# A seven-product form for one more projection of an encoder trunk, and a new order of the kernel's last five stages

## The chip, the cores and the metric

The kernel runs on one core of a Trainium2 chip. The metric is the time on the device, in microseconds (us), as the median of several runs. The engines are TensorE (PE, matrix products), VectorE (DVE, element-wise work), ScalarE (ACT, element-wise work and copies), GpSimd (POOL) and SyncE (SP, which issues all the transfers here).

## What is computed

One layer of a bidirectional encoder for a prompt of 1024 tokens and a sample of 512 tokens, 1024 channels, everything in 32-bit floats. `_hgrn2_bidir` is a gated linear recurrence in both directions over 8 heads of 128 channels, with a norm of each head.

```python
h = _rmsnorm(x, norm_g)
proj = jnp.einsum('bld,de->ble', h, w_in)
(q, f_fw, f_bw, i, z_a, c_B, c_C, c_x, z_b, g_a, g_b) = jnp.split(proj, SPLIT_POINTS, axis=-1)
o_a = _hgrn2_bidir(q, i, f_fw, f_bw, lb_fw, lb_bw, hnorm_g).astype(x.dtype)
p_a = jnp.einsum('ble,ed->bld', o_a * jax.nn.silu(z_a), w_a)
conv = _centred_short_conv(c_C * c_x, conv_w, conv_b)
p_b = jnp.einsum('ble,ed->bld', c_B * conv * jax.nn.silu(z_b), w_b)
merged = jax.nn.sigmoid(g_a) * p_a + jax.nn.sigmoid(g_b) * p_b
return x + jnp.einsum('bld,de->ble', merged, w_o)      # then a final RMSNorm
```

The first branch is `p_a` (weights `w_a`), the second `p_b` (weights `w_b`).

## The kernel before

**Products.** Each 32-bit operand is split into two parts of type fp32r: `split` (L61) has ACT copy the high part (`w_h` of a weight block, `s_h` of activations) and then DVE subtract it from the source (`w_l`, `s_l`). A product is three passes, high by high, high by low, low by high (`PASSES`, L34). A plain product of a block of 128 channels with 512 tokens is 8 x 3 = 24 matmuls of 128x512 into one bank of PSUM (`mm_channels`, L90, its matmul L94). A *unit* is one such product for the sample, with the loading and splitting of its weight block done up to three units ahead.

**Seven products for eight.** For two blocks of channels and two halves of the prompt (or, in the output, of the columns), `two_blocks` (L766) forms seven products of half the depth, 12 matmuls each (L781), in place of four whole ones (4 x 24). It needs sums of the weights (`S`, four DVE operations L792 to L797, then splits), and sums of the other operand: B11, B21 and B22 are quarters of it, T1 to T4 sums of quarters. Those seven are made once for a stage by `operands` (L709), four steps of loads, subtractions and splits, and lie in seven slots of SBUF (`s0` to `s6`), each a high and a low part. The products' sums are added on DVE (`c`, `sum`).

**The stages.** The norm, values and the prompt's projections take the first 885 us. Then comes the recurrence (the GLA loop, L662): for each of 8 heads three steps, the prompt's two blocks and the sample (`order`, L653). In a step PE computes the scores of the block before (`near_scores`, L447 its matmuls; `transpose_keys`, L496), while DVE, ACT and POOL make the decays of the next (`decays`, K and Q on L433 and L434, `cat` on L431 and L432). Between the pieces stand units of the sample's projections, three in each step (L678, L684, L689), so nine for a head. `outputs` (L521) uses a single bank of PSUM: matmuls L533, squares on ACT L537, a sum on DVE L538, a power on POOL, a scaling on ACT L541 that frees the bank. The prompt's outputs come in two halves, with one unit between them. The order of PE in the loop is that of the code.

After the loop, a `while` loop (L901) issues the units that are left, and between them the first steps of the next operands. The order from there, by a scheduler within each engine: the sample's `w_b` (plain), the prompt's `w_b` (seven products), the prompt's `w_a` (plain, two halves of 512 tokens for each of 8 blocks), the sample's `w_a` (plain), the output with `w_o` (seven products, six pairs of token blocks). In a plain stage `weights_ahead` (L815) loads and splits weight blocks three ahead and takes a step of the following stage's operands after every second block.

```python
        O = {n: slot(qp, i) for i, n in ((2, "T1"), (3, "T2"), (4, "T4"))}
        act = act_parts(cz_x[1], slot(qp, 5), slot(qp, 6))
        ...
        O |= {"B11": slot(keep, 0), "T3": slot(keep, 1)}
        ...
        O |= {"B21": slot(qp, 5), "B22": slot(qp, 6)}
```

Slots 0 and 1 (`keep`) hold the normed sample during the loop and the units behind it, so what is put there waits for the last of those units.

Of the kernel before, what the change touches and what calls it, by code (L numbers as in the profile page):

```python
# [10 lines left out]
F32 = mybir.dt.float32  # L11
# [3 lines left out]
ALU = mybir.AluOpType  # L15
# [3 lines left out]
P = 128  # L19
D = 1024  # L20
# [23 lines left out]
def trunk_kernel(ctx: ExitStack, tc: tile.TileContext, xs, w, outs, masks_d, ident_d):  # L44
# [330 lines left out]
    with outer:  # L375
# [286 lines left out]
        for i in range(len(order) + 1):  # L662
# [26 lines left out]
            unit()  # L689
# [16 lines left out]
        qp, io = opened(outer, "qp", bufs=1), opened(outer, "io", bufs=4)  # L706
# [50 lines left out]
        def products(O, srcs, use, early=False):  # L757
# [75 lines left out]
        def branch_b_prompt(O):  # L833
            s = {}

            def srcs(i):
                js = range(2 * i, min(2 * i + 2, NH))
                for j in js:
                    yield w["w_b"][:, j * P:(j + 1) * P].rearrange("(k p) c -> p k c", p=P)
                for j in js:  # L840
                    s[j] = io.tile([P, 2, TB], F32, name="io")
                    load(s[j].rearrange("p a b -> p (a b)"), gb_x[0][j])

            def use(i, m, t, c, more):
# [3 lines left out]
                V.tensor_tensor(s[m][:, t, :], u, s[m][:, t, :], op=ALU.mult)  # L848
                if m % 2 != t:
                    store(pb_x[0][m], s[m].rearrange("p a b -> p (a b)"))  # L850
# [3 lines left out]
        def branch_a(blocks, x, acts):  # L854
            n = len(acts)
            for j, whl in blocks:
                if n == 1:
                    both = io.tile([P, 2, TB], F32, name="io")
                    s, s2 = both[:, 0, :], both[:, 1, :]
                else:  # L860
                    s, s2 = (io.tile([P, n * TB], F32, name="io") for _ in range(2))
                load(s, ga_x[x][j])
                load(s2, pb_x[x][j])
                for t in range(n):
                    cols = slice(t * TB, (t + 1) * TB)
                    V.tensor_tensor(s[:, cols], plain(whl, acts[t]), s[:, cols], op=ALU.mult)
                V.tensor_tensor(s, s, s2, op=ALU.add)
                store(m_x[x][j], s)

        def output(O):  # L870
            xt, ss = {}, {}
# [9 lines left out]
            def use(i, m, h, c, more):  # L881
# [5 lines left out]
                if m != h:  # L887
# [7 lines left out]
            products(O, srcs, use, early=True)  # L895

        rows = lambda k: cz_x[0][k]
        O = {n: slot(qp, i) for i, n in ((2, "T1"), (3, "T2"), (4, "T4"))}
        act = act_parts(cz_x[1], slot(qp, 5), slot(qp, 6))
        steps = operands(O, tuple(O), rows)  # L900
# [6 lines left out]
        O |= {"B11": slot(keep, 0), "T3": slot(keep, 1)}  # L907
        blocks = weights_ahead("w_b", steps + operands(O, ("B11", "T3"), rows))
        next(blocks)
        branch_b_sample(blocks, act)  # L910
        O |= {"B21": slot(qp, 5), "B22": slot(qp, 6)}
        for step in operands(O, ("B21", "B22"), rows):
            step()
        stage = ExitStack()
        wk = opened(stage, "wk", bufs=1, side="right")
        branch_b_prompt(O)
        stage.close()

        xp = opened(stage, "xp", bufs=1, side="right")
        rows = lambda k: w["w_o"][k * P:(k + 1) * P, :]  # L920
        steps = []
        blocks = weights_ahead("w_a", steps)
        next(blocks)
        acts = [act_parts(oz_d[0], slot(keep, 0), slot(qp, 3)), act_parts(oz_d[1], slot(keep, 1), slot(qp, 2))]
        O = {"T4": slot(qp, 4), "T1": slot(qp, 5), "T2": slot(qp, 6)}
        steps += operands(O, tuple(O), rows)
        branch_a(blocks, 0, acts)
        steps = []
# [46 lines left out]
```

## Time and profile before

| | |
|---|---|
| median of 3 runs | 1977.19 us |
| lowest, highest | 1972.35, 1985.93 us |
| the profiled execution | 1982.88 us |
| its span in the trace | 1981.1 us |
| stages in the trace: GLA loop | 885 to 1576 us |
| units left over, `w_b` of the sample | 1576 to 1643 us |
| `w_b` of the prompt | 1643 to 1723 us |
| `w_a` of the prompt, of the sample | 1723 to 1811, to 1855 us |
| output | 1855 to 1981 us |

The profile is of one execution. Busy time of a matmul in it counts from its start to its modelled end, and matmuls overlap; the pitch, from one start to the next, is what a matmul costs. An engine's idle time is put down to the instruction that released it. A name such as `w_l<-w_raw,w_h` gives an instruction's output and inputs; the last three columns of a window are the clock granted to TensorE as a share of full speed, the busy share of the DMA engines and GB/s; `io` are tiles for loads and stores of stages, `pw` and `pp` PSUM banks.

### The profile page before, as it was taken

The page shows a single profiled execution, that of the slowest core. Times are in us where ns is not written, and L with a number is a line of the kernel's source. Part 1 is how long each engine was busy: PE and PEld are TensorE (multiplying, and loading weights), DVE is VectorE, ACT ScalarE, POOL GpSimd, SP SyncE. Part 2 cuts the span into 40 slices and gives each one's busy share as a digit, 9 for nine tenths or more (in the row PEclk, how much of TensorE's full clock was granted, in tenths as well). Part 3 has the DMA queues.
Part 4 walks back from the last instruction along what each step waited for, and adds up shares of the span by engine and source line. Part 5 has one row for each costly group of instructions (what it writes and reads, how often), then busy time and mean ns, then how long its engine had stood idle before and what let it go on. Part 6 is the DMA issues. An engine that isn't in the chain of part 4 may idle for free.

```text
span 1981.1 us, 37160 instructions
## 1 busy us (share of the span) xinstructions
PE 1940.3 (98%) x14820; PEld 1633.4 (82%) x14820; DVE 1476.4 (75%) x2369; ACT 981.5 (50%) x1956; POOL 170.2 (9%) x220
## 2 busy tenths in 40 slices
PE   9999999999999999998999999999999999999998
PEld 8988888888888888886888888888888887888786
DVE  6558686878676777776688878879788378765687
ACT  6433333343424333345677877877877443332332
POOL 1000000000000000003121322322212000000000
PEclk8999999999999999998999999999999999999999
DMA  7433333333324242435443534434333497798653
GB/s 214 146 108 103 115 96 107 102 120 97 120 88 131 77 138 75 128 113 184 146 124 118 161 112 128 142 106 156 110 120 104 143 308 254 241 313 278 214 186 107
DMA packets 313757, 288.85 MB, mean 146 GB/s; under 512 B 19184, under 2 KB 252912, under 8 KB 313584
## 3 DMA queue, kind: packets, MB, share of 16 engines
q1 hardware_dynamic: 313584, 286.49, 45.8%
q8 instruction: 116, 1.90, 0.4%
q14 instruction: 57, 0.47, 0.1%
HBM read 208.84 MB, written 77.59 MB: 145 GB/s over the span
## 4 chain that ended last, share of the span: by engine, by line
PE 77%; issue 9%; DVE 5%; DMA 5%; ACT 3%; POOL 1%; SPq 0%; DVEq 0%; POOLq 0%; ACTq 0%
PE pp L309 38%; PE pp L94 16%; PE pw L781 9%; PE pp L215 5%; PE o L533 2%; PE pp L87 2%; PE sc L447 2%; DMA io<-in_w_o 1%; PE u L509 1%; DVE Q L434 1%; DVE K L433 1%; ACT cat L431 1%; DVE w_l L64 1%; DMA w_raw<-in_w_b 1%; PE tp L177 1%
## 5 line engine op out<-in xcount | busy, mean ns | idle before, releaser
L309 PE MATMUL pp<-s_h,w_h 128*128 128x512 f32 x1120 | 435.9, 389 | 1.2 <-ACT w_h L63 1.2
L309 PE MATMUL pp<-s_l,w_h 128*128 128x512 f32 x1120 | 435.7, 389 | 0.0
L309 PE MATMUL pp<-s_h,w_l 128*128 128x512 f32 x1120 | 435.7, 389 | 0.0
L63 ACT ACTIVATE w_h<-w_raw 128x1024 fp32r<-128x1024 f32 (+1 forms) x250 | 209.6, 838 | 323.4 <-PE pp L309 137.8
L94 PE MATMUL pp<-s_h,w_h 128*128 128x512 f32 x896 | 356.5, 398 | 0.0
L94 PE MATMUL pp<-s_h,w_l 128*128 128x512 f32 x896 | 350.0, 391 | 1.5 <-DVE w_l L64 1.5
L94 PE MATMUL pp<-s_l,w_h 128*128 128x512 f32 x896 | 350.0, 391 | 0.2 <-DVE s_l L64 0.2
L64 DVE TENSOR_TENSOR w_l<-w_raw,w_h 128x1024 fp32r<-128x1024 f32 (+1 forms) x250 | 238.4, 954 | 101.0 <-ACT w_h L63 99.4
L314 DVE TENSOR_TENSOR tmp<-pp,tmp 128x512 f32<-128x512 f32 x240 | 165.3, 689 | 156.1 <-PE pp L309 156.1
L309 PEld LDWEIGHTS pp<-s_h,w_h 128*128 128x128 f32 x1120 | 210.2, 188 | 45.3 <-ACT w_h L63 1.8
L309 PEld LDWEIGHTS pp<-s_l,w_h 128*128 128x128 f32 x1120 | 210.2, 188 | 43.6
L309 PEld LDWEIGHTS pp<-s_h,w_l 128*128 128x128 f32 x1120 | 210.2, 188 | 43.6
L63 ACT ACTIVATE w_h<-w_S 128x512 fp32r<-128x512 f32 x160 | 101.0, 632 | 263.4 <-PE pp L309 263.3
L94 PEld LDWEIGHTS pp<-s_h,w_l 128*128 128x128 f32 x896 | 168.6, 188 | 38.3 <-DVE w_l L64 2.3
L94 PEld LDWEIGHTS pp<-s_l,w_h 128*128 128x128 f32 x896 | 168.9, 189 | 34.1 <-DVE s_l L64 1.0
L94 PEld LDWEIGHTS pp<-s_h,w_h 128*128 128x128 f32 x896 | 169.2, 189 | 33.0 <-ACT w_h L63 0.3
L431 ACT COPY cat<-K 128x512 f32<-128x512 f32 x168 | 111.6, 668 | 36.8 <-DVE K L433 35.4
L433 DVE TENSOR_TENSOR K<-K,T 128x512 f32<-128x512 f32 x144 | 110.1, 764 | 18.7 <-ACT cat L431 17.4
L432 ACT COPY cat<-Q 128x512 f32<-128x512 f32 x168 | 111.4, 668 | 19.4 <-DVE Q L434 10.8
L434 DVE TENSOR_TENSOR Q<-Q,T 128x512 f32<-128x512 f32 x144 | 104.0, 722 | 16.2 <-ACT cat L432 15.5
L781 PE MATMUL pw<-s_h,w_h 128*128 128x512 f32 x280 | 110.6, 395 | 2.5 <-ACT w_h L63 2.5
L781 PE MATMUL pw<-s_h,w_l 128*128 128x512 f32 x280 | 110.5, 395 | 1.1 <-DVE w_l L64 1.1
(178 smaller groups left out, 2961.5 us busy)
## 6 DMA issues: line engine op xcount, KB each, us to landing
w_raw<-in_w_in SPq DMA_DIRECT2D x166, 512.0 KB, 4.4
fkq_d<-sg SPq DMA_DIRECT2D x48, 256.0 KB, 2.3
io<-cz_p SPq DMA_DIRECT2D x20, 512.0 KB, 5.4
fkq_d<-sk SPq DMA_DIRECT2D x32, 256.0 KB, 2.1
F<-fkq_d SPq DMA_DIRECT2D x16, 512.0 KB, 3.7
K<-fkq_d SPq DMA_DIRECT2D x16, 512.0 KB, 6.5
w_raw<-in_w_b SPq DMA_DIRECT2D x16, 512.0 KB, 4.8
w_raw<-in_w_a SPq DMA_DIRECT2D x16, 512.0 KB, 6.1
```

The source lines that it names most:

```text
L63: A.activation(hi, src, AF.Copy)
L64: V.tensor_tensor(lo, src, hi.bitcast(F32), op=ALU.subtract)
L87: T.matmul(out, lhs(k, a), parts[k // 2][b][:, k % 2, :], start=k == 0 and n == 0, stop=k == KT - 1 and n == 2)
L94: T.matmul(out, whl[a][:, k, :], rhs(k, b), start=k == 0 and n == 0, stop=k == KT - 1 and n == 2)
L215: T.matmul(pp, B[f"B{k // 4 + 1}{t + 1}"][a][:, k % 4, c * P:(c + 1) * P], parts[k][b], start=k == 0 and m == 0, stop=k == KT - 1 and m == 2)
L309: T.matmul(bank, hl[x][:, k, :], B[b][y][:, k, :], start=k == 0 and i == 0, stop=k == 3 and i == 2)
L314: V.tensor_tensor(out, p, t, op=ALU.add)
L431: A.copy(ap(cat, 0, [[2 * hs, nb], [hs, 2], [1, hs]]), kall)
L432: A.copy(ap(cat, TB, [[2 * hs, nb], [hs, 2], [1, hs]]), qall)
L433: V.tensor_tensor(kall, kall, ap(t, m + 1, [[2, nb], [-m - 1, 2], [0, hs]]), op=ALU.mult)
L434: V.tensor_tensor(qall, qall, ap(t, 1, [[2, nb], [m - 1, 2], [0, hs]]), op=ALU.mult)
L781: T.matmul(bank, hl[x][:, c:c + P], O[n][y][:, k, :], start=k == 0 and i == 0, stop=k == 3 and i == 2)
```

## The change

1. The prompt's `w_a` takes the seven-product form: 4 pairs x 7 x 12 = 336 matmuls of 128x512, where 384 stood. Gate and second branch are applied to each half block (`branch_a_prompt`).
2. In the GLA loop the third unit of a step is left out in the sample's step (`i % 3 < 2`), so a head has eight units. The eight units go to the `while` loop behind it, which has 12 left where it had 4; the list of units is dealt out by fours accordingly.
3. The last five stages stand in this order: the prompt's `w_b`, the sample's `w_b`, the prompt's `w_a`, the sample's `w_a`, output. A seven-product stage has its first five operands (`FIRST`) made during the stage before and the last two (`LAST`: B21 and B22) at that stage's end, in slots that the stage before still reads.
4. In `two_blocks`, the product with B21 comes last but one in the first pair of a stage and second in the later ones; the output had it second in all, `w_b` last but two in all.
5. `io` has 8 tiles (4 before), `wk` is opened once, and the ring in SBUF for descriptors (`dynamic_dma_scratch_size`) is set to 2048.

```diff
-            units += [narrow(n, h) for n in ("q", "ff", "fb", "za")] + [wide(0)] * (h == 0) + later[5 * h:5 * h + 5]
-        units += later[5 * NH:]
+            units += [narrow(n, h) for n in ("q", "ff", "fb", "za")] + [wide(0)] * (h == 0) + later[4 * h:4 * h + 4]
+        units += later[4 * NH:]
...
-            unit()
+            if i % 3 < 2:
+                unit()
...
-        qp, io = opened(outer, "qp", bufs=1), opened(outer, "io", bufs=4)
+        qp, io = opened(outer, "qp", bufs=1), opened(outer, "io", bufs=8)
...
-                raws = two_blocks(O, *raws, partial(use, i), early, partial(srcs, i + 1))
+                raws = two_blocks(O, *raws, partial(use, i), i > 0, partial(srcs, i + 1))
...
+            use(1, 0, c21, prod(last, 0, "T4"))
             if not early:
                 use(0, 0, c11, prod(first, 1, "B21"))
-            use(1, 0, c21, prod(last, 0, "T4"))
             use(0, 1, c12, prod(s34, 1, "B22"))
...
+        def branch_prompt(name, O, finish_block, pb=None):
+
             s = {}
 
             def srcs(i):
                 js = range(2 * i, min(2 * i + 2, NH))
                 for j in js:
-                    yield w["w_b"][:, j * P:(j + 1) * P].rearrange("(k p) c -> p k c", p=P)
+                    yield w[name][:, j * P:(j + 1) * P].rearrange("(k p) c -> p k c", p=P)
                 for j in js:
                     s[j] = io.tile([P, 2, TB], F32, name="io")
-                    load(s[j].rearrange("p a b -> p (a b)"), gb_x[0][j])
+                    load(s[j].rearrange("p a b -> p (a b)"), (gb_x if name == "w_b" else ga_x)[0][j])
+                    if name == "w_a":
+                        pb[j] = io.tile([P, 2, TB], F32, name="io")
+                        load(pb[j].rearrange("p a b -> p (a b)"), pb_x[0][j])
...
+        def branch_a_prompt(O):
+            pb = {}
+
+            def block(m, t, s, u):
+                V.tensor_tensor(u, u, s[:, t, :], op=ALU.mult)
+                V.tensor_tensor(s[:, t, :], u, pb[m][:, t, :], op=ALU.add)
+                left_of[m] = left_of.get(m, 0) + 1
+                if left_of[m] == 2:
+                    store(m_x[0][m], s.rearrange("p a b -> p (a b)"))
+
+            left_of = {}
+            branch_prompt("w_a", O, block, pb)
...
+        FIRST, LAST = ("B11", "T1", "T2", "T3", "T4"), ("B21", "B22")
+        wk = None
+
+        def first_operands(slots, rows):
+            O = dict(zip(FIRST, slots))
+            return O, operands(O, FIRST, rows)
+
+        def last_operands(O, slots, rows):
+            O |= dict(zip(LAST, slots))
+            for step in operands(O, LAST, rows):
+                step()
...
         rows = lambda k: cz_x[0][k]
...
+        O, steps = first_operands(take(2, 3, 4, 5, 6), rows)
         while todo or ready:
             unit()
             if steps:
                 steps.pop(0)()
         order_pe.close()
         right.close()
...
+        wk = opened(outer, "wk", bufs=1, side="right")
+        fg = wk.tile([P, D], F32, name="fg")
+        load(fg, w["final_g"].to_broadcast([P, D]))
+        last_operands(O, take(0, 1), rows)
+        branch_b_prompt(O)
+
+        rows = lambda k: oz_x[0][k]
+        act = act_parts(cz_x[1], *take(2, 4))
+        O, steps = first_operands(take(5, 3, 6, 0, 1), rows)
+        blocks = weights_ahead("w_b", steps)
         next(blocks)
         branch_b_sample(blocks, act)
...
+        last_operands(O, take(2, 4), rows)
+        branch_a_prompt(O)
+
         rows = lambda k: w["w_o"][k * P:(k + 1) * P, :]
...
+        act = act_parts(oz_x[1], *take(5, 6))
+        O, steps = first_operands(take(0, 1, 2, 3, 4), rows)
         blocks = weights_ahead("w_a", steps)
         next(blocks)
...
+        branch_a_sample(blocks, act)
+        last_operands(O, take(5, 6), rows)
         output(O)
```

Two places show how instructions move. The first is ACT at the start of the output. `s0_h` to `s6_h` are the slots' high parts (of `w_o`'s operands), `io` the loaded rows of `w_o`, `S` the sums of the merged activations and `w_raw` those activations as loaded. Before:

```order
L63 ACTIVATE s0_h_18813<-io_19107 128x512 [waits DMAHW1_49]
L63 ACTIVATE s3_h_18817<-io_19109 128x512 [waits DMAHW3_49]
L63 ACTIVATE s2_h_18819<-io_19109 128x512
L63 ACTIVATE s1_h_18815<-io_19107 128x512 [waits DVE_49]
L63 ACTIVATE w_h_19208<-S_19167 128x1024 [waits DVE_49,PE_49,Activation_49]
L789 COPY c_19168<-pw_19175 128x512 [waits PE_49]
L63 ACTIVATE w_h_19228<-S_19167 128x1024 [waits DVE_49,Activation_49]
```

And after the change:

```order
L63 ACTIVATE s5_h_19235<-io_19239 128x512 [waits DMAHW1_49,PE_49]
L63 ACTIVATE s4_h_18865<-io_19188 128x512 [waits DVE_49]
L63 ACTIVATE s5_h_19235<-io_19245 128x512 [waits DMAHW2_49]
L63 ACTIVATE s5_h_19235<-io_19251 128x512 [waits DMAHW3_49]
L63 ACTIVATE s6_h_19237<-io_19239 128x512 [waits PE_49]
L63 ACTIVATE s6_h_19237<-io_19245 128x512
L63 ACTIVATE s6_h_19237<-io_19251 128x512
L63 ACTIVATE s5_h_19235<-io_19257 128x512 [waits DMAHW5_49]
L63 ACTIVATE s6_h_19237<-io_19257 128x512
L63 ACTIVATE w_h_19277<-w_raw_19263 128x1024 [waits DMAHW6_49,Activation_49]
L63 ACTIVATE w_h_19297<-S_19273 128x1024 [waits DVE_49,Activation_49]
L63 ACTIVATE w_h_19317<-S_19273 128x1024 [waits DVE_49,Activation_49]
```

Before, the first `w_h` of the output stood further ahead, and only splits for slots 0 to 3 came before the `w_h` of `S`; none of those splits waits for PE. Now eight splits for slots 5 and 6, B21 and B22, stand ahead of the first `w_h<-w_raw`, and the first for each slot waits for PE, which reads them as the sample's operand of `w_a`.

The second place is DVE at the start of the prompt's `w_b`, where slots hold parts of the second branch's `cz`, loaded into `io`. Before, at the end of the sample's `w_b` (L830 applies its gate):

```order
L64 TENSOR_TENSOR s0_l_17223<-io_17504,s0_h_17222 128x512 [waits DMAHW5_49,Activation_49]
L726 TENSOR_TENSOR io_17504<-io_17506,io_17504 128x512 [waits DMAHW7_49,DMAHW1_49]
L64 TENSOR_TENSOR s1_l_17225<-io_17504,s1_h_17224 128x512 [waits Activation_49]
L792 TENSOR_TENSOR S_17581<-w_raw_17575 128x512 [waits DMAHW0_49]
L796 TENSOR_TENSOR S_17581<-w_raw_17573,w_raw_17575 128x512
L793 TENSOR_TENSOR S_17581<-S_17581,w_raw_17573 128x512 [waits DVE_49]
L830 TENSOR_TENSOR io_17513<-pp_17515,io_17513 128x512 [waits DMAHW6_49,DMAHW2_49,PE_49]
L797 TENSOR_TENSOR S_17581<-w_raw_17573,S_17581 128x512 [waits DVE_49]
L64 TENSOR_TENSOR w_l_17606<-S_17581,w_h_17605 128x1024 [waits Activation_49]
```

And after the change, behind the units left over:

```order
L64 TENSOR_TENSOR s0_l_17224<-io_17245,s0_h_17223 128x512 [waits DMAHW2_49,Activation_49]
L64 TENSOR_TENSOR s1_l_17226<-io_17227,s1_h_17225 128x512 [waits PE_49,Activation_49]
L64 TENSOR_TENSOR s1_l_17226<-io_17233,s1_h_17225 128x512 [waits Activation_49]
L64 TENSOR_TENSOR s1_l_17226<-io_17239,s1_h_17225 128x512 [waits Activation_49]
L64 TENSOR_TENSOR s1_l_17226<-io_17245,s1_h_17225 128x512 [waits Activation_49]
L794 TENSOR_TENSOR S_17259<-w_raw_17253 128x512 [waits DMAHW7_49,Pool_49]
L798 TENSOR_TENSOR S_17259<-w_raw_17251,w_raw_17253 128x512
L795 TENSOR_TENSOR S_17259<-S_17259,w_raw_17251 128x512 [waits DVE_49]
L799 TENSOR_TENSOR S_17259<-w_raw_17251,S_17259 128x512 [waits DVE_49]
L64 TENSOR_TENSOR w_l_17284<-S_17259,w_h_17283 128x1024 [waits Activation_49]
```

Before, the `S` sums stood behind the last splits of slots 0 and 1 (B11 and T3) and ahead of the last gate of the sample, and slots 5 and 6 (B21, B22) came behind them. Now the splits of slots 0 and 1, which are B21 and B22 here, all stand ahead of the `S` sums, and those of slot 1 wait for PE's last unit.

## Rows read from the trace of the kernel before

**Rows 1.** The page: busy time, share and instructions of each engine.

```profile
PE 1940.3 (98%) x14820; PEld 1633.4 (82%) x14820; DVE 1476.4 (75%) x2369; ACT 981.5 (50%) x1956; POOL 170.2 (9%) x220
```

**Rows 2.** By stage: us; busy PE, PEld, DVE, ACT, POOL; clock, DMA share, GB/s.

```profile
885.00:1576.00 691.00, 669.12 (x8852) 566.94 (x8851) 536.21 (x883) 499.07 (x1152) 155.05 (x192) 0.98 0.43 132
...
1643.00:1723.00 80.00, 78.07 (x337) 63.85 (x336) 62.30 (x90) 29.52 (x42) 0.00 (x0) 0.98 0.67 227
...
1855.00:1981.00 126.00, 116.50 (x505) 95.29 (x503) 101.61 (x156) 42.01 (x80) 7.76 (x12) 0.97 0.46 154
```

**Rows 3.** Waits of PE: us in total, times, longest.

```profile
PE o L533 <- ACT oz L541: 14.1, 7, 2.1
...
PE pw L781 <- ACT w_h L63: 2.5, 2, 1.4
...
PE pp L94 <- DVE w_l L64: 1.5, 2, 0.9
...
PE pw L781 <- DVE w_l L64: 1.1, 2, 0.5
```

**Rows 4.** Timeline of PE at the start of w_b for the prompt.

```profile
1645.39 0.39 PE L781 MATMUL pw<-s_h,w_l 128*128 128x512 f32 x1
...
1648.44 0.64 PE L781 MATMUL pw<-s_h,w_l 128*128 128x512 f32 x1 [0.53 <-DVE w_l L64]
1648.88 0.63 PE L781 MATMUL pw<-s_h,w_h 128*128 128x512 f32 x1
1649.31 0.63 PE L781 MATMUL pw<-s_l,w_h 128*128 128x512 f32 x1
```

**Rows 5.** Windows behind a wait at the output's start and behind one in the loop.

```profile
1863.20:1867.00 3.80, 3.80 (x11) 2.98 (x10) 2.71 (x5) 1.03 (x3) 0.00 (x0) 0.56 1.00 364
1247.40:1251.40 4.00, 4.00 (x29) 3.74 (x30) 3.24 (x4) 3.51 (x8) 1.07 (x3) 1.00 0.16 57
```

**Rows 6.** Windows in the plain stages.

```profile
1620.00:1632.00 12.00, 12.00 (x54) 9.95 (x53) 7.38 (x9) 4.93 (x6) 0.00 (x0) 1.00 1.00 324
1710.00:1815.00 105.00, 104.76 (x461) 86.19 (x460) 71.25 (x96) 34.13 (x49) 0.00 (x0) 1.00 0.88 296
```

**Rows 7.** Windows of one head of the loop, in three parts.

```profile
1358.50:1380.90 22.40, 22.40 (x338) 18.77 (x337) 20.88 (x38) 15.97 (x33) 5.28 (x7) 1.00 0.50 161
...
sum 78.00, PE 75.98 PEld 64.67 DVE 65.14 ACT 60.00 POOL 19.90; mean PE 25.33 PEld 21.56 DVE 21.71 ACT 20.00 POOL 6.63
```

**Rows 8.** Timeline of DVE in that head.

```profile
1373.19 0.69 DVE L434 TENSOR_TENSOR Q<-Q,T 128x512 f32<-128x512 f32 x1
...
1389.46 1.23 DVE L64 TENSOR_TENSOR w_l<-w_raw,w_h 128x1024 fp32r<-128x1024 f32 x1 [1.05 <-ACT w_h L63]
```

**Rows 9.** Timelines of ACT and PE between the head's first and second outputs.

```profile
1396.48 0.27 ACT L537 ACTIVATE oz<-o 128x128 f32<-128x128 f32 x1
...
1401.64 0.49 PE L533 MATMUL o<-v,pt 128*128 128x128 f32 x2 [2.02 <-ACT oz L541]
```

**Rows 10.** Groups by form, 1570 to 1981 us: DVE, ACT, ACT; then DVE's timeline.

```profile
L64 DVE TENSOR_TENSOR w_l<-w_raw,w_h 128x1024 fp32r<-128x1024 f32 x35 | 42.7, 1221 | 12.6 <-ACT w_h L63 12.5
...
L63 ACT ACTIVATE w_h<-w_raw 128x1024 fp32r<-128x1024 f32 x35 | 37.1, 1059 | 70.4 <-PE pp L94 24.4 <-PE pw L781 14.9 <-issue 11.5
L63 ACT ACTIVATE s_h<-io 128x512 fp32r<-128x512 f32 x56 | 34.2, 628 | 74.1 <-DVE io L726 44.3 <-DMA io<-in_w_o 22.2 <-DMA io<-cz_p 7.3
...
1856.09 1.89 DVE L64 TENSOR_TENSOR s_l<-io,s_h 128x512 fp32r<-128x512 f32 x3
```

**Rows 11.** Timeline of PE at the output's start.

```profile
1860.13 0.39 PE L781 MATMUL pw<-s_h,w_l 128*128 128x512 f32 x1
...
1862.87 0.50 PE L781 MATMUL pw<-s_h,w_l 128*128 128x512 f32 x1 [0.53 <-DVE w_l L64]
```

**Rows 12.** DMA: packets, MB and share of the main queue; w_o's loads, us to landing.

```profile
q1 hardware_dynamic: 313584, 286.49, 45.8%
...
io<-in_w_o SPq DMA_DIRECT2D x16, 512.0 KB, 5.4
```

More of the change, by code (lines that the diff above doesn't have):

```diff
@@ L755, in raw_block, with products @@
             return raw
-        def products(O, srcs, use, early=False):
+        def products(O, srcs, use):
             raws = [raw_block(x) for x in srcs(0)]
@@ L847, in use, with branch_b_prompt, block, branch_a_sample @@
                 V.tensor_tensor(u, more, c, op=ALU.add)
-                V.tensor_tensor(s[m][:, t, :], u, s[m][:, t, :], op=ALU.mult)
-                if m % 2 != t:
-                    store(pb_x[0][m], s[m].rearrange("p a b -> p (a b)"))
+                finish_block(m, t, s[m], u)
             products(O, srcs, use)
-        def branch_a(blocks, x, acts):
-            n = len(acts)
-            for j, whl in blocks:
[L857 to L866, printed above, removed]
+        def branch_b_prompt(O):
+            left_of = {}
+            def block(m, t, s, u):
+                V.tensor_tensor(s[:, t, :], u, s[:, t, :], op=ALU.mult)
+                left_of[m] = left_of.get(m, 0) + 1
+                if left_of[m] == 2:
+                    store(pb_x[0][m], s.rearrange("p a b -> p (a b)"))
+            branch_prompt("w_b", O, block)
+        def branch_a_prompt(O):
+            pb = {}
+            def block(m, t, s, u):
+                V.tensor_tensor(u, u, s[:, t, :], op=ALU.mult)
+                V.tensor_tensor(s[:, t, :], u, pb[m][:, t, :], op=ALU.add)
+                left_of[m] = left_of.get(m, 0) + 1
+                if left_of[m] == 2:
+                    store(m_x[0][m], s.rearrange("p a b -> p (a b)"))
+            left_of = {}
+            branch_prompt("w_a", O, block, pb)
+        def branch_a_sample(blocks, act):
+            for j, whl in blocks:
+                both = io.tile([P, 2, TB], F32, name="io")
+                s, s2 = both[:, 0, :], both[:, 1, :]
+                load(s, ga_x[1][j])
+                load(s2, pb_x[1][j])
+                V.tensor_tensor(s, plain(whl, act), s, op=ALU.mult)
                 V.tensor_tensor(s, s, s2, op=ALU.add)
-                store(m_x[x][j], s)
+                store(m_x[1][j], s)
         def output(O):
-            xt, ss = {}, {}
+            xt, ss, halves = {}, {}, {}
             def srcs(i):
@@ L893, in use @@
                         store(o_tiles[n][:, cols], x)
-            products(O, srcs, use, early=True)
+            products(O, srcs, use)
+        FIRST, LAST = ("B11", "T1", "T2", "T3", "T4"), ("B21", "B22")
[7 more added lines that the diff above has]
+                step()
+        at = {i: (keep if i < 2 else qp, i) for i in range(7)}
+        take = lambda *ns: [slot(*at[n]) for n in ns]
         rows = lambda k: cz_x[0][k]
-        O = {n: slot(qp, i) for i, n in ((2, "T1"), (3, "T2"), (4, "T4"))}
-        act = act_parts(cz_x[1], slot(qp, 5), slot(qp, 6))
-        steps = operands(O, tuple(O), rows)
+        O, steps = first_operands(take(2, 3, 4, 5, 6), rows)
         while todo or ready:
```

33 lines of the change are left out of this document (3 added, 30 removed).

## The prediction

> **What bounds the kernel now.** I began with the page's busy line [rows 1]: TensorE (PE) is busy for 1940.3 of 1981.1 us, VectorE (DVE) for 75% and ScalarE (ACT) for 50%, so only PE's work, its idle 41 us and its clock can move the time. Then the stretches of the program [rows 2]: the GLA loop (885 to 1576 us) has 22 us of idle, the first seven-product stage of the end 1.9, and the output stage 9.5, most of it behind its last matmul. PE's waits [rows 3] name the idle: seven waits of up to 2.1 us before the second half of a head's outputs (14.1 us), and at the starts of the two seven-product stages 2.5 us for ACT's w_h and 1.1 us for DVE's w_l. Last I looked at the clock after such waits. Matmuls of 128x512 follow each other at 0.228 us (461 in 105.00 us, [rows 6]). At the start of w_b for the prompt PE gets from 1645.39 to 1648.44 with two matmuls between, and then eight come 0.43 us apart, the first at 1648.88 and 1649.31 [rows 4], before the pace is 0.23 again. The window after the output's start shows a granted clock of 0.56, for most of it the lower of the two levels (1.2 GHz of 2.4); one after a 2 us wait of the loop shows 1.00 [rows 5]. Of the loop's seven waits five were followed by such a dip. So a dip costs 8 x 0.2 = 1.6 us on top of its wait.
>
> The profiled execution took 1982.88 us, 0.3% above the median of 1977.19 us. I make the sum against the profiled execution and put its difference on the median. A difference below about 1% can't be told from none here, since the three runs lie 0.7% apart.
>
> **1. Matmuls taken out.** w_a for the prompt was 8 blocks x 2 halves x 24 = 384 matmuls; it is now 4 pairs x 7 products x 12 = 336. 48 fewer, at the stretch's pitch: 461 in 105.00 us is 0.228 us [rows 6], so **-10.9 us**. The added work lies on DVE. The model for it is w_b's prompt stage, with PE at 78.07 and DVE at 62.30 of 80.00 us [rows 2]; w_a adds one 0.69 us addition for each of 16 half blocks, 11 us, and so has 73 us of DVE beside 336 x 0.228 = 76.5 of PE. PE still sets the pace, narrowly (rival d).
>
> **2. One unit less per head in the GLA loop.** Eight units of 24 matmuls move behind the loop: the same matmuls at the same pitch, 0 of PE work. What changes is cover. Between the scores of the prompt's second block (1358.5) and those of the sample (1380.9), PE had 22.40 us of work with DVE busy for 20.88 [rows 7]; without the unit it is 17.0 us. The unit takes a split of 1.22 us [rows 10] and one or two 0.7 us uses away from DVE, which leaves 18.3 to 19.0 us of DVE for 17.0 us of PE. The sample's last decay K and Q ended at 1373.9 [rows 8], 7 us before PE asked for them; now the margin is about 1.6 us plus the split taken out, some 3 us. So no stall there, but DVE arrives up to 2 us later. It has idle gaps after that, behind ACT's copies and splits, the longest 1.05 us and 3.9 us in all up to the squares' use [rows 8], which take some of it up. The wait that it can lengthen is the one before the second outputs [rows 9]: they need the only PSUM bank of the first, which ACT frees after squares that begin at 1396.48, a sum on DVE and a scaling; PE goes on at 1401.64 after 2.02 us of idle. Nothing in the trace shows a loop with eight units. Bounds: -22 (the seven waits go, 14.1, and their five dips, 8) and +37 (each of eight heads gets a wait of 3 us and a dip of 1.6). I take 0.5 us a head, a quarter of those 2 us, since those gaps are longer than the lateness: **+4 us**.
>
> **3. Start of w_b for the prompt.** It now follows the leftover units directly. Its B21 and B22 go into slots that those units read until their last matmul, and on DVE they stand ahead of the S sums (second order listing). From PE's end of the last unit: four s_h for B22 at 0.63 us each and the s_l behind them end at 3.1 us, four S operations at 0.63 (three such in 1.89 us) end at 5.6, w_h of S (1.06, on ACT after the third of them) at 6.1, w_l (1.22) at 7.4 [rows 10]. PE has 14 matmuls until it needs that w_l, 3.2 us. Lost: 4.2 and a dip, 5.8 us. Before, the same place cost 1648.44 - 1645.39 - 0.8 = 2.25 and the dip, 3.9 [rows 4].
>
> **4. Start of the output.** B21 and B22 of w_o are now loaded and split in the last blocks of w_a, and on ACT they all stand ahead of the first w_h (first listing); before, nothing there waited for the end of the sample's matmuls. The last of the four loads is queued on SP behind the store of block 6, some 3 us before PE's end, and needs 5.4 us [rows 12]: it lands 2.4 us after PE's end. Two s_h (1.3) and w_h (1.06) make the first matmul possible at 4.8 us [rows 10]. DVE then does w_l (1.22), the S sums (2.5) and, after ACT's w_h, w_l of S (1.22): the third matmul of T2 comes at 10.1 us, where 14 matmuls would have come by 3.2. Lost: 6.9 and a dip, 8.5 us; 5.7 and a dip if the load is early. Before, 1862.87 - 1860.13 - 0.8 = 1.95 and a dip, 3.6 [rows 11].
>
> **5. The other starts.** w_b for the sample and w_a for the prompt have their first splits or S sums ahead of those that wait for PE: 0. At w_a for the sample DVE does sum (after the last product of the pair before) ahead of the first w_l of 1.22: 1.5 us and half a dip, 2.3. Before, plain starts waited 1.5 us for w_l in two places [rows 3], 0.5 us of it among these stages, and 0.2 for an s_l: 0.8 with rounding up.
>
> Terms 3 to 5: 5.8 + 8.5 + 2.3 = 16.6 against 8.3 before, so **+8.3 us** (between 5, with the load early and one dip less, and 11, with dips twice as long at the two long waits).
>
> The Trainium skill speaks against this part: "TensorE: Matmul & The Clock Gate", section "What's actually happening", says that the throttled clock is the default and that activity releases it, so a change that puts new idle into stage starts pays twice. The trace agrees at both starts of seven products (0.43 us apart; clock 0.56) and not everywhere (1.00 at 1247.4); by the rule taken without exception the half dip of w_a is a whole one, 0.8 us more.
>
> **6. Transfers.** The sample's w_a stage moves w_a (4.2 MB), w_o (6.3), its own operand, gate and w_b part (6.3) and its result (2.1): 18.9 MB in about 55 us. By 324 GB/s, the rate at a full DMA share [rows 6], that is 58 us; by 364 GB/s in another full window [rows 5] it is 52. So 0 to +3 us for it, and as much for the sample's w_b, which moves less. With twice the io buffers loads start earlier, which speaks for the low end: **+1.5 us**, bounds 0 and 8.
>
> The Trainium skill, "DMA: Bandwidth & Descriptors", section "Where 436 GB/s comes from", puts the limit of a core's HBM at about 358 GB/s; the estimate from that page is 53 us, no stall, and the sum would be 1.5 us lower. The trace's 364 lies at it.
>
> The smaller scratch for descriptors and the earlier B21 product of each later pair I cost at nothing: the 286.49 MB of before all went by one queue, hardware_dynamic [rows 12], and the matmuls are only reordered.
>
> **Sum.** -10.9 + 4 + 8.3 + 1.5 = **+2.9 us**: 1985.8 on the profiled basis, 1977.19 + 2.9 = **1980 us** on the median's.
>
> **Rivals.**
> (a) The loop gets faster. With one split and one use per head less in ACT's and DVE's queues, the squares start sooner and the waits before the second outputs go with their dips: -22 in place of +4, 1954 us. For it: the wait ends with ACT's chain, 2.6 us of which lie between PE's outputs and the first square [rows 9]. Against: DVE's surplus goes the other way. Half of it gives 1965.
> (b) The loop becomes bound by DVE: the sample's K and Q come after PE asks for them. It decides from a DVE lateness of 3 us on, the margin of step 2; each head then pays some 3 + 1.6 us, +37 in place of +4: 2013 us, and 1995 at half. For it: 18.3 to 19.0 us of DVE in 17.0 of PE. Against: the whole head has DVE busy for 65 of 78 us [rows 7], so it can't fall further behind from head to head.
> (c) Transfers bind in both sample stages: +8 in place of 1.5, and the output's last load lands later still: 1987 us.
> (d) DVE sets the pace of w_a for the prompt. If the eight splits of the sample's operand (8 x 0.69 = 5.5 us [rows 10]) fall into it as well, DVE has 78.8 us for PE's 76.5: 2.3 us lost and a dip in each of four pairs, +9 in all: 1989 us. Against: DVE's durations overlap, three took 1.89 us from start to end [rows 10], so the 78.8 are nearer to 72.
>
> **How the numbers follow.** My forecast has 0.46, (c) 0.12 and (d) 0.12, all three between 1965 and 1995; (a) in full or nearly so has 0.14, (b) 0.16. Same, within 1957.4 to 1997.0, holds the first three and the weak ends of the others: **0.74**; faster **0.13**, slower **0.13**. The range leaves out the full (a) and (b): half of (a) with the starts at their low end is 1962, half of (b) with transfers 2 us dearer 1997.
>
> **What would show it.** In the changed trace: 14772 matmuls in place of 14820, some 11 us less PE work at equal clock; the loop shorter by about 8 x 5.4 - 4 = 39 us and the leftover stretch longer by 43; a first wait of about 4 us for w_h or w_l in w_b for the prompt and about 5 us ahead of the output's first matmul, each with a dip to about 0.55; waits for oz of 2 to 3 us, eight times. I am wrong if the oz waits vanish or pass 4 us, or if the output's first matmul follows the last one of w_a at once.

## The result, and the profile after the change

The changed kernel took 1997.22 us as the median of nine runs (1986.37 to 1998.99); the kernel before took 1978.82 us (nine runs, 1972.35 to 1985.93). The ratio is 1.0082, 95% interval 1.0061 to 1.0103: slower, by some 16 us, and inside the 1% that was called "same". The forecast of 1980 us was 13 to 17 us low; the median lies 0.2 us past the end of the range (1997.0), and the ratio on the median shown before, 1977.19, gives 1993.4, inside it.

The profiled execution is the fastest of the nine, 1986.37 us with a span of 1984.6. So the trace shows 3.5 us more than the trace of before, not 16. First the page's busy line of the changed kernel, which answers to [rows 1]:

```profile
span 1984.6 us, 37157 instructions
...
PE 1926.7 (97%) x14772; PEld 1622.8 (82%) x14772; DVE 1524.8 (77%) x2457; ACT 997.3 (50%) x1980; POOL 167.9 (8%) x220
```

48 matmuls fewer, PE busy for 13.6 us less, and the span longer: the idle time of PE went from 41 to 58 us. The windows by stage (loop; units left over; w_b of the prompt; w_a of the prompt; w_a of the sample with the wait behind it; output) say where:

```profile
885.00:1539.00 654.00, 622.34 (x8653) 528.10 (x8652) 522.42 (x868) 486.47 (x1137) 153.26 (x192) 0.98 0.43 130
1539.00:1605.00 66.00, 66.00 (x294) 54.66 (x294) 40.45 (x58) 29.66 (x44) 0.00 (x0) 1.00 0.70 239
1605.00:1688.60 83.60, 79.60 (x337) 64.84 (x336) 60.83 (x89) 27.95 (x37) 0.00 (x0) 0.96 0.56 183
...
1732.20:1808.30 76.10, 76.10 (x337) 63.05 (x336) 67.10 (x101) 25.16 (x35) 0.00 (x0) 1.00 0.75 256
1808.30:1860.00 51.70, 43.76 (x194) 35.89 (x193) 47.58 (x73) 22.49 (x34) 0.00 (x0) 0.97 0.93 308
1860.00:1984.00 124.00, 116.58 (x504) 95.57 (x504) 99.42 (x150) 41.32 (x77) 7.29 (x12) 0.97 0.43 144
```

The prompt's w_a takes 76.10 us with PE busy for all of it, where the plain form had 384 matmuls in some 88: the gain came in full. The loop has 31.7 us of idle in place of 22 [rows 2]; w_b for the prompt 4.0 in place of 1.9, and 7.9 us stand ahead of the output. The waits of PE, which answer to [rows 3]:

```profile
PE o L533 <- ACT oz L541: 16.0, 7, 4.1
PE pw L783 <- ACT w_h L63: 11.9, 2, 7.9
PE u L496 <- DVE oz L548: 9.9, 7, 2.6
```

Two of the three lines are as forecast in kind: longer waits for w_h at the two starts, and the waits before the second outputs still 2 us a head, but for 4.1 us in the first, which passes the 4 us that the prediction had named as a sign of being wrong. The third is new and was not forecast. Its place is the sample's step, here in the third head, PE's timeline and then DVE's:

```profile
1129.68 0.60 PE L547 MATMUL u<-ident,oz 128*128 128x128 f32 x4
...
1131.46 0.55 PE L496 MATMUL u<-ident,K 128*128 128x128 f32 x3
1134.01 0.55 PE L496 MATMUL u<-ident,K 128*128 128x128 f32 x3 [2.00 <-DVE oz L548]
```

```profile
1130.87 1.16 DVE L433 TENSOR_TENSOR K<-K,F 128x512 f32<-128x512 f32 x1
1131.88 1.48 DVE L518 SCALAR_TENSOR_TENSOR us<-us,T 128x128 f32<-128x128 f32 x4
1133.27 0.68 DVE L548 TENSOR_TENSOR oz<-u,zg 128x512 f32<-128x512 f32 x1
```

`finish` transposes the sample's oz into one of the two PSUM buffers called u (L547, done by 1130.3); DVE's multiply that empties it (L548) stands behind decays and states and ends at 1133.95; the next step's key transposes need that buffer, and without the unit of 5.4 us between them PE arrives at 1132 and waits.

The start of the output, PE's timeline and then ACT's:

```profile
1851.63 0.39 PE L94 MATMUL pp<-s_h,w_l 128*128 128x512 f32 x1
1859.97 0.79 PE L783 MATMUL pw<-s_h,w_h 128*128 128x512 f32 x1 [7.94 <-ACT w_h L63]
1860.56 0.63 PE L783 MATMUL pw<-s_l,w_h 128*128 128x512 f32 x1
```

```profile
1856.98 1.15 ACT L63 ACTIVATE s_h<-io 128x512 fp32r<-128x512 f32 x2 [1.22 <-DMA io<-in_w_o]
1858.86 1.06 ACT L63 ACTIVATE w_h<-w_raw 128x1024 fp32r<-128x1024 f32 x1 [0.73 <-DMA w_raw<-m_p]
```

ACT waits for the last load of w_o with two splits, then for the activations themselves, and only then makes the w_h that PE waits for. The matmuls behind it come 0.43 us apart at first, the lower clock (1.2 GHz of 2.4), as behind the start of w_b (a window of 0.61, with one of 0.66 here). Before, the same place had two short waits and one dip [rows 5, 11]. In the loop a dip follows the wait before the second outputs in every second head, four in all (before, it was five of seven), and none starts behind a wait of the new kind:

```profile
1156.00:1165.00 9.00, 9.00 (x167) 7.72 (x166) 6.23 (x11) 5.75 (x18) 3.04 (x4) 0.92 0.44 118
...
1229.00:1236.00 7.00, 7.00 (x155) 5.73 (x154) 5.07 (x9) 4.43 (x17) 3.04 (x4) 1.00 0.54 150
1303.00:1312.00 9.00, 9.00 (x167) 7.70 (x167) 6.11 (x11) 5.63 (x18) 3.03 (x4) 0.93 0.43 117
1611.80:1620.00 8.20, 8.08 (x22) 5.96 (x23) 3.65 (x4) 1.49 (x3) 0.00 (x0) 0.61 0.93 298
1859.90:1866.00 6.10, 5.99 (x17) 4.34 (x18) 5.56 (x7) 2.91 (x5) 0.00 (x0) 0.66 0.79 297
```

**The rest of the 16 us** is in the executions that were not traced in full. Each has a span and a mean granted clock, so span x (1 - clock) is the time lost to the slow clock, and span x clock is the rest (work at full speed, and idle). The split isn't clean: the granted clock is counted also while PE stands idle, so some of the first part is no slow matmul (4.5 us in the trace of before, 4.6 us in that of the changed kernel). Over the runs of one chip, six of the changed kernel and twelve of before (`a_again`, below): mean span 1991.7 against 1975.9; lost to the clock 26.6 against 18.6; rest 1965.1 against 1957.3. So the change costs 7.8 us of idle and work, and as much again, 8.0 us, of clock. The two profiled executions hide this: before's (clock 0.988 of 1981.1) lost 23.8 us, more than the mean of its runs, and the changed one's (0.989 of 1984.6) lost 21.8, less than the mean of its own. What they show of the clock is 3.4 us more lost at the starts of w_b for the prompt and of the output together (6.8 against 3.4) and 3.4 less in the loop (10.2 against 13.6).

### The profile page after: what moved, and what is told of

It reads as the page before. It is cut to its first block, busy times and chain, and to the rows that moved or that the text cites. A ratio compares the mean times of both kernels' runs of the same rounds, so it can differ in the third digit from the quotient of the medians.

```text
span 1984.6 us, 37157 instructions
## 1 busy us (share of the span) xinstructions
PE 1926.7 (97%) x14772; PEld 1622.8 (82%) x14772; DVE 1524.8 (77%) x2457; ACT 997.3 (50%) x1980; POOL 167.9 (8%) x220
## 4 chain that ended last, share of the span: by engine, by line
PE 75%; issue 10%; DVE 8%; ACT 3%; DMA 3%; POOL 1%; SPq 0%; DVEq 0%; POOLq 0%; ACTq 0%
PE pp L309 38%; PE pw L783 13%; PE pp L94 12%; PE pp L215 5%; DVE Q L434 2%; PE o L533 2%; PE pp L87 2%; DVE K L433 2%; DVE w_l L64 1%; PE sc L447 1%; DMA io<-in_w_o 1%; ACT w_h L63 1%; POOL rs_o L98 1%; ACT cat L432 1%; PE tp L177 1%
## 5 line engine op out<-in xcount | busy, mean ns | idle before, releaser
L309 PE MATMUL pp<-s_h,w_h 128*128 128x512 f32 x1120 | 435.9, 389 | 1.2 <-ACT w_h L63 1.2
L309 PE MATMUL pp<-s_l,w_h 128*128 128x512 f32 x1120 | 435.8, 389 | 0.0
L309 PE MATMUL pp<-s_h,w_l 128*128 128x512 f32 x1120 | 435.7, 389 | 0.0
L94 PE MATMUL pp<-s_h,w_h 128*128 128x512 f32 x768 | 305.5, 398 | 0.0
L94 PE MATMUL pp<-s_h,w_l 128*128 128x512 f32 x768 | 299.6, 390 | 0.9 <-DVE w_l L64 0.9
L94 PE MATMUL pp<-s_l,w_h 128*128 128x512 f32 x768 | 299.4, 390 | 0.0
L309 PEld LDWEIGHTS pp<-s_h,w_h 128*128 128x128 f32 x1120 | 210.2, 188 | 45.4 <-ACT w_h L63 1.8
L309 PEld LDWEIGHTS pp<-s_h,w_l 128*128 128x128 f32 x1120 | 210.2, 188 | 43.7
L309 PEld LDWEIGHTS pp<-s_l,w_h 128*128 128x128 f32 x1120 | 210.2, 188 | 43.5
L94 PEld LDWEIGHTS pp<-s_h,w_l 128*128 128x128 f32 x768 | 144.4, 188 | 32.0 <-DVE w_l L64 1.4
L94 PEld LDWEIGHTS pp<-s_l,w_h 128*128 128x128 f32 x768 | 144.9, 189 | 28.2
L94 PEld LDWEIGHTS pp<-s_h,w_h 128*128 128x128 f32 x768 | 144.8, 189 | 27.8
L783 PE MATMUL pw<-s_h,w_h 128*128 128x512 f32 x392 | 154.8, 395 | 11.9 <-ACT w_h L63 11.9
L783 PE MATMUL pw<-s_l,w_h 128*128 128x512 f32 x392 | 154.3, 394 | 0.0
L783 PE MATMUL pw<-s_h,w_l 128*128 128x512 f32 x392 | 154.2, 394 | 0.1
```

The costliest lines, as they stand in the source:

```text
L94: T.matmul(out, whl[a][:, k, :], rhs(k, b), start=k == 0 and n == 0, stop=k == KT - 1 and n == 2)
L309: T.matmul(bank, hl[x][:, k, :], B[b][y][:, k, :], start=k == 0 and i == 0, stop=k == 3 and i == 2)
L783: T.matmul(bank, hl[x][:, c:c + P], O[n][y][:, k, :], start=k == 0 and i == 0, stop=k == 3 and i == 2)
```

## The experiments

The table has, for each run, the ratio to the kernel before and by how much the mean span differs from that of before on the same chip, split in the same way. The clock is given in thousandths, so a part is good to about 1 us; and an idle stretch at the lower clock stands half in either part.

| run | ratio, 95% interval | span, us | by clock | rest |
|---|---|---|---|---|
| `a_again` | 1.0080, 1.006 to 1.010 | +15.8 | +8.0 | +7.8 |
| `e1_unit_kept` | 1.0055, 1.0039 to 1.0071 | +10.8 | +11.2 | -0.4 |
| `e3_last_late` | 1.0042, 1.0026 to 1.0058 | +8.3 | +4.9 | +3.4 |
| `e4_finish_first` | 1.0093, 1.0074 to 1.0111 | +18.9 | +9.7 | +9.2 |
| `e5_unit_step0` | 1.0088, 1.0070 to 1.0107 | +17.3 | +7.9 | +9.4 |
| `e6_step0_late` | 1.0053, 1.0038 to 1.0068 | +10.2 | +6.1 | +4.1 |
| `e7_units_only` | 1.0065, 1.0048 to 1.0083 | +12.0 | +3.4 | +8.6 |
| `e8_io4` | 1.0197, 1.0178 to 1.0216 | +38.7 | +17.2 | +21.5 |
| `e9_bank_o` | 1.0057, 1.0044 to 1.0071 | +11.1 | +10.2 | +0.9 |
| `e10_all_three` | 0.9988, 0.9976 to 1.0000 | -2.5 | +3.3 | -5.8 |
| `e11_four_heads` | 0.9939, 0.9916 to 0.9962 | -12.0 | -1.8 | -10.1 |
| `e12_two_heads` | 0.9961, 0.9946 to 0.9977 | -7.6 | +0.4 | -8.0 |

**The changed kernel again** (no edit).

> The changed kernel once more, for the trace of another execution; its first profiled execution (1986.4 us) was the fastest of nine, the median 1997. Theory (clock): the waits are the same as in the first trace within 1 us each (transposes behind oz about 10 us, second outputs behind oz about 16, w_h about 12), and an execution near 1995 has its 10 us more as matmuls at half the clock, in the GLA loop. Rival (transfers): the waits themselves vary, above all the one ahead of the output's first matmul (7.9 us), by 5 us or more, and the clock is the same. Time 1990 to 1999.

The three main waits came within 1.1 us of the first trace (17.1, 11.5, 10.4 us), so the rival fell: the wait ahead of the output is 7.5 us here and 7.9 there. The span of this trace is 5.6 us more. The clock lost 1990.2 x 0.013 = 25.9 us, against 21.8, but part of that is idle at the lower clock: PE's whole idle time is 62.0 us against 57.9, about 1.5 us of the difference in the first 50 us of the program. The dips in the loop stand in every second head too. So the theory, that the time goes to matmuls in the loop, isn't shown by this execution. No execution of the changed kernel above 1995 us was traced, so where those lose their further 6 us stays open; their recorded clock of 0.984 to 0.985 says that the clock has most of it.

**The unit back in the loop.**

```diff
-            units += [narrow(n, h) for n in ("q", "ff", "fb", "za")] + [wide(0)] * (h == 0) + later[4 * h:4 * h + 4]
+            units += [narrow(n, h) for n in ("q", "ff", "fb", "za")] + [wide(0)] * (h == 0) + later[5 * h:5 * h + 5]
...
-            if i % 3 < 2:
-                unit()
+            unit()
```

> The changed kernel with the third unit of the sample's step put back into the GLA loop, everything else as changed. Theory (the missing unit uncovers the transposes, which wait for the multiply that frees their PSUM bank): the wait of the transposes (9.9 us) is gone, the loop takes what it took before, and the time is 8 to 16 us below the changed kernel, 1981 to 1989; the waits for w_h at the two starts stay at about 12 us. Rival (the end is what costs): at most 3 us below the changed kernel, about 1993.

```profile
PE pw L782 <- ACT w_h L63: 23.0, 2, 15.0
PE o L533 <- ACT oz L541: 14.1, 7, 2.1
...
1605.90:1623.00 17.10, 5.77 (x13) 4.13 (x14) 13.34 (x20) 6.15 (x10) 0.00 (x0) 0.50 0.82 280
```

The loop went back to what it took before, and the wait of the transposes is gone. But the wait at the start of w_b for the prompt grew from 4.0 to 15.0 us: four units don't cover the making of five operands that twelve had covered. The window shows how the table's split misleads here: the clock was at its lower level for 17.1 us, in which PE worked for 5.8, so some 5.7 of the 11.2 us "by clock" are idle time. The mean span fell by 5.0 us, less than expected, and half the expectation failed: the moved units are a trade, dearer in the loop, needed behind it.

**The last operands' splits later.**

```diff
             s34, last = parts(S[:, 1, :]), parts(a22)
+            if not early:
+                late()
```

where `late` makes the splits for B21 and B22; the first weights are loaded ahead of those operands, and the first pair's S sums and splits have high priority in the scheduler.

> The changed kernel with the splits of B21 and B22 issued behind the first pair's S sums in each seven-product stage (their loads behind the first weights' loads). Theory (those splits, queued on ACT ahead of the first w_h, make the 7.9 us wait of the output): that wait falls below 2 us and the time by 6 to 9 us, to 1986 to 1991. Rival (the load of w_o lands late anyway): the wait moves to the products with B21 and B22, and the time falls by less than 3 us. At the start of w_b for the prompt the S sums use memory that the loop's pools give back late, so little changes there by either (4.0 us before).

```profile
PE pw L784 <- ACT w_h L63: 4.4, 2, 4.0
```

The waits for w_h went from 11.9 us to 4.4, of which 4.0 is the start of w_b as said (there this run's trace still has the splits ahead of the S sums), and the time fell by 7.5 us of mean span. The rival, that the load is late anyway, fell: no wait for B21 or B22 appeared. Since the loads and the splits moved together, it doesn't tell how much of the 7.9 us either had.

**The finish ahead of the unit.**

```diff
+            if to_finish and i % 3 == 2:
+                finish(to_finish)
+                to_finish = None
             unit()
```

> The changed kernel with the finish of the sample's outputs (transposes of oz, multiply by the gate) ahead of the second unit of the sample's step instead of behind it. Theory (the bank, uncovered): a unit of 5.4 us then covers the multiply, the wait of the key transposes (9.9 us) falls below 2 us with its share of slow clock, and the time falls by 8 to 16 us, to 1981 to 1989. Rival (VectorE is simply late by then): the wait comes back elsewhere, at the sample's K and Q or before the second outputs (16 us now, then 22 or more), and the time stays within 3 us.

```profile
PE pw L786 <- ACT w_h L63: 13.0, 2, 9.0
PE u L547 <- ACT us L510: 12.1, 6, 2.5
```

The rival held in kind: the wait came back, at a place that neither thought had named. The transposes of keys no longer wait, but those of oz now do, for the copies that empty the same two buffers after the contributions. It cost as much as before: in both orders the two uses of the pair that lost the unit between them got the wait.

**Another unit left out**, in the step of a head's first block (`if i % 3:` in place of `if i % 3 < 2:`), and that together with the late splits.

> The changed kernel with the unit left out of the GLA loop in another place: behind the second outputs in the step of a head's first block, instead of behind the sample's finish; as many units as changed in the loop and behind it. Theory (place: the wait comes where VectorE and ScalarE have no slack and the two-buffer bank of the transposes is used twice in a row): the 10 us of waits on that bank, for oz or for us, vanish, and no other wait of the loop grows by more than 3 us in all; time 8 to 13 us below the changed kernel, 1982 to 1987. Rival (any unit less uncovers as much): a new wait of 8 us or more in the step of the first block, time as changed, 1990 to 1997.

> The unit left out as in the run before this one and the late splits of B21 and B22 together. Theory (two separate causes that add): both gains, 15 to 22 us below the changed kernel, 1971 to 1979, which is the kernel before or better. Rival (they share the same slow clock, or the loop does not gain): 1982 to 1988.

The rival held in the first: waits of the transposes for oz (6.2 us over ten places), a time as changed, and the one wait for K at the loop's start, 4.4 us in the changed kernel, now 8.0. Of the two places tried neither was cheaper. In the second the late splits gave 7 us, as they had in `e3_last_late`, and the loop gave nothing back, so the time lies in the rival's range.

**The loop's part alone**, on the kernel before.

```diff
-        later = [wide(1)] + [narrow(n, h) for h in range(NH) for n in ("cx", "cC", "cB", "zb", "gb")]
-        later += [narrow("ga", h) for h in range(NH)]
+        later = [wide(1)] + [narrow(n, h) for h in range(NH) for n in ("cx", "cC", "cB", "zb")]
+        later += [narrow(n, h) for n in ("gb", "ga") for h in range(NH)]
...
-            unit()
+            if i % 3 < 2:
+                unit()
+            left += 1
+            if left == 2:
+                act = act_parts(cz_x[1], slot(qp, 5), slot(qp, 6))
```

> The kernel before with the loop's part of the change alone: one unit less in the sample's step of each head, eight more behind the loop (the gate units of the second branch come later in the list, and the sample's operand is split behind the second unit that is left, so that it is there). Theory (the loop change by itself costs): the waits of the transposes for oz appear, about 10 us, the average clock falls, and the time is 8 to 14 us above the kernel before, 1986 to 1992. Rival (the loop is neutral and the end costs): within 3 us of before, 1975 to 1981.

```profile
PE u L496 <- DVE oz L548: 8.5, 6, 1.9
```

It shows the waits of the transposes for oz and costs 12.0 us, 8.6 of them not by the clock: as expected, and three quarters of the 15.8 us that the changed kernel loses in all.

**Four io tiles** (`bufs=4`).

> The changed kernel with four io tiles, as before, instead of eight. Theory (the output's first weights and the last loads of w_o queue behind buffers anyway; transfers do not bind the sample's stages): the wait for w_h ahead of the output grows by at most 2 us and the time by less than 4. Rival (transfers bind with fewer buffers): waits in the plain stages of the end and 6 to 15 us more.

Both thoughts were too small: 23 us more than the changed kernel. The windows of its w_a stages, prompt and sample, show it:

```profile
1740.00:1833.00 93.00, 82.24 (x338) 64.54 (x336) 75.10 (x113) 27.85 (x40) 0.00 (x0) 0.96 0.72 230
1833.00:1880.00 47.00, 46.10 (x191) 37.32 (x190) 37.40 (x53) 17.19 (x23) 0.00 (x0) 0.93 0.91 287
```

The prompt's w_a takes 93 us in place of 76 with the DMA engines busy for 0.72 of it, less than the 0.75 of the changed kernel, so the mean rate of transfer is not the limit. By the code a pair takes four tiles for its gate and second branch, which leaves none for the next pair's; that this is the whole cause was not tried apart.

**Another PSUM buffer for the sample's finish.**

```diff
-                p = bank("u", 2)
+                p = bank("u", 2) if g.n == 8 else bank("o", 1)
```

> The changed kernel with the sample's finish (transposes of oz, multiply by the gate) in the single PSUM buffer of the outputs, which is free at that time, instead of one of the two that the key transposes and the contributions share; order and everything else as changed. Theory (the shared buffers are what the missing unit uncovers): the transposes' wait for oz (10 us) is gone and the multiply's lateness hurts nobody; the loop loses 10 us or less of idle and the time is 7 to 13 us below the changed kernel, which two measurements put at 1.0080 to 1.0082 of before; here 0.9995 to 1.005 of before. Rival (VectorE's lateness itself; whatever waits first is replaced by the next): other waits grow by 6 us or more, at K, cat or the second outputs, and the ratio stays at 1.006 or above.

```profile
PE o L533 <- ACT oz L541: 22.8, 7, 4.9
PE pw L783 <- ACT w_h L63: 13.3, 2, 9.3
PE u L496 <- DVE K L433: 4.1, 1, 4.1
```

Between the two. The transposes' wait is gone, and the rest fell by 6.9 us; but two thirds of the wait came back before the second outputs (22.8 in place of 16 to 17 us), and the clock lost as much as before. PE's idle time in this trace, 58.8 us, lies between the 57.9 and 62.0 of the changed kernel's two. So the buffers are the first place where the lateness of VectorE and ScalarE shows, and behind them it shows in the next.

**Three repairs together**, the third with the S sums of w_b's first pair in two io tiles (`S = [io.tile(...) for _ in range(2)]`).

> Three changes to the changed kernel together: the sample's finish in the outputs' PSUM buffer, the late splits of B21 and B22, and the S sums of the first pair of w_b for the prompt in two io tiles, so that they need no memory of the loop's pools and can be made during the last units. Theory (each new wait has its own cause, and the 48 matmuls saved are then left over): the waits for w_h at the two starts fall from 12 us to below 3, the loop's new waits are gone, and the time is 0.990 to 0.998 of before. Rival (the loop's waits come back elsewhere): 1.000 to 1.004 of before.

```profile
PE o L533 <- ACT oz L541: 22.6, 7, 4.8
PE pw L788 <- ACT w_h L63: 2.6, 2, 2.1
```

The waits for w_h fell to 2.6 us, all of it at the output; at the start of w_b, where the S sums now stand ahead of the splits on DVE, none is left. So each start's cause is shown. The loop's waits before the second outputs stayed at 22.6, as the rival had it. The ratio falls between the two forecasts: of the 10.9 us of the 48 matmuls 2.5 are left over.

**The unit left out in every second head, and in two heads.**

```diff
-            if i % 3 < 2:
+            if i % 3 < 2 or i // 3 not in (1, 3, 5, 7):
```

> The three changes together, and the unit left out of the loop in every second head only, so that eight units in place of twelve stand behind the loop. Theory (what a head loses in the loop is paid per unit left out, and eight units are still enough cover for the operands of w_b for the prompt): waits for oz of 2 us in the heads with nine units, no wait over 2 us at the start of w_b, and 3 to 8 us less than with all heads short, 0.994 to 0.998 of before. Rival (eight units don't cover the operands, as four did not): a wait of 4 us or more for w_h at that start, and the ratio stays at 0.999 or above.

> The same with the unit left out in two heads only, six units behind the loop. Theory (cover runs out between eight and four units): the loop gains another 2 us, a wait of 3 to 8 us for w_h comes at the start of w_b for the prompt (15 us with four units), and the ratio is 0.996 to 1.001. Rival (six are enough): wait below 2 us, ratio 0.992 to 0.996.

The second run has `(3, 7)`; the list of units is dealt out to match. Both went as the theory had it, the first further: 9.5 us of mean span less than with all heads short, where 3 to 8 were expected. With eight units behind the loop no wait stands at the start of w_b, and the time is 1967.94 us, the ratio 0.9939: faster than both kernels. With six, a wait of 4.0 us stands there again and the ratio is 0.9961; with four it had been 15.0, in a kernel without the repairs. PE's waits with eight:

```profile
PE o L533 <- ACT oz L541: 17.1, 7, 4.1
PE u L496 <- DVE K L433: 4.6, 1, 4.6
PE pw L788 <- DVE w_l L64: 1.8, 4, 0.6
```

## Why the prediction was right and wrong

**Term 1** was right: -10.9 us forecast, 76.1 us in place of some 88 measured, and PE without a wait, so rival (d) did not come.

**Term 2** had its sign and a wrong size and place. I argued that DVE would arrive up to 2 us late and that this would lengthen the wait before the second outputs by 0.5 us a head: +4. The lateness came (the multiply ended 2 us after PE wanted its buffer), but at the key transposes, since I had followed K and Q and the outputs' buffer and not the pair of buffers that `finish`, the transposes and the contributions share. It was dearer: 8.6 us without the clock and 12.0 with it (`e7_units_only`), about 1.5 us a head. `e9_bank_o` shows that my place was the next one in line.

**Terms 3 and 4** were right to between 1 and 2 us each, and their causes are shown by `e10_all_three` and `e3_last_late`. At w_b: 83.6 us for 336 matmuls, which at 0.228 take 76.6, so 7.0 lost against 5.8; the steps were as told, with the wait at w_h of the S sums. At the output: one wait of 7.94 us and a dip of about 2 against 6.9 and 1.6. Here the steps were not as told, and the size owes something to luck: the first matmul came 8 us after PE's end and not 4.8, since w_o's last load and the activations landed late, and then nothing waited for the S sums. **Term 5** was not there: w_a for the sample began without a wait. **Term 6** was 0 in the changed kernel, and what I named as its hint, the doubled io buffers, is worth 23 us: the cover that I thought a margin was a condition.

Together the terms give +2.9 us, and the two traces differ by 3.5. That is luck: by the traces it is -11.6 of PE's work at full clock (its busy time less what the clock lost), +17.1 of idle and -2.0 of clock. **The step that failed** is the one from there to the median: "I make the sum against the profiled execution and put its difference on the median." I took the dips that stood in one execution as the kernel's own. The trace of before had lost 23.8 us to the clock, the mean of its runs 18.6, and I let the changed one keep that and add about one dip; measured, the changed kernel loses 26.6, 8 us more than before. With that, and the loop at 8.6, the sum is -11.6 + 8.6 + 8.3 + 8.0 = +13; the 8.3 are the waits at the two starts, 11.9 against 2.5 + 1.1 before [rows 3]. That leaves some 3 of the 16 us without a name, or more, since idle at the lower clock is counted twice in it. Where the clock loses 8 us more stays open in part: 3.4 are seen at the starts, and the rest in no trace. It goes with the waits, though: +8.0 here, +3.3 with the starts mended (`e10_all_three`), -1.8 with the unit back in every second head as well (`e11_four_heads`). That the ratio still lies within 1% is a near thing.

**The rule weighed in the prediction**, that of the Trainium skill ("TensorE: Matmul & The Clock Gate", "What's actually happening") that activity releases the throttle, has the direction of the result: the changed kernel's 7.8 us went with another 8.0 of clock. The trace shows no fixed price for a wait: of the seven before the second outputs four were followed by a dip and three, of 1.9 to 2.0 us, were not, and behind the seven new ones at the transposes, of up to 2.6 us, none started.

## What to carry to other kernels

A unit of independent PE work between two uses of a small set of PSUM buffers is cover for the engines that empty them, so before moving it, list every wait that it hides, buffer by buffer, and not only those for data. Filler is worth most where it covers something: nine units a head and four behind left a wait of 15 us at the next start, eight and twelve cost 9 us in the loop, and a split between the two was the best of those tried. And where a kernel's executions differ by 0.7% in themselves, one trace on each side can hide a change of that size; spans and clocks of all runs separate what the traces don't.

## What was not expected of the hardware

The granted clock of one and the same program varies between executions: 0.984 to 0.989 over nine runs of the changed kernel, spans of 1997.2 to 1984.6 us, although the three main waits in two traces agree within 1.1 us each. And waits of equal length don't cost equal clock: behind the 2.0 us waits before the second outputs, heads with a window of 0.92 or 0.93 and heads with 1.00 take turns. In the heads with the dip the wait at the transposes some 19 us earlier is the longer one (2.0 to 2.6 us, where the others have 0.6 to 1.3); whether it has a part in this isn't shown, and before, without such waits, five heads of seven had the dip.
